# A casting load issued at the head of the kernel instead of inside its loop: 3x3 convolution by row-Winograd on one core

## The chip, the cores and the metric

The kernel runs on one core of a Trainium2 chip. The metric is the device time of one execution, in microseconds. The profile adds one profiled execution, read by its span (from the first to the last instruction) and by what each engine and each transfer queue did in it. Engines are named as in the profile: PE (TensorE), DVE (VectorE), ACT (ScalarE), POOL (GpSimd) and SP (SyncE, which here only issues transfers).

## The reference

A 3x3 convolution with padding 1. The input has 16 images of 64 channels, 64 x 64 pixels, the output 16 images of 128 channels, all float32.

```python
batch, c_in, h, w, c_out = 16, 64, 64, 64, 128
x_pad = np.pad(x, ((0, 0), (0, 0), (1, 1), (1, 1)), mode='constant')
# for every image b, output channel co, input channel ci, kh, kw in 0..2:
output[b, co] += weight[co, ci, kh, kw] * x_pad[b, ci, kh:kh+h, kw:kw+w]
```

The input is 16.8 MB and the output 33.6 MB.

## The kernel before

**Tiling.** Two images are worked on together. A pair's input is one tile of 128 partitions (2 images x 64 channels) by 64 x 64 pixels, and there are eight pairs, numbered 0 to 7. Two output rows are computed together: with the weight rows G0, G1, G2 of the filter, the products of G1 with the sum of two neighbouring input rows (`ss`, fp16) are common to both, and the combined weights G2-G1 and G0-G1 make up the rest from the input rows themselves (`xs`, fp16). Each pair is done in four blocks of eight row pairs. In a block, PE makes three groups of products (L150): U from `ss`, then A and B from `xs`, each for both images. ACT copies U from PSUM (L164), DVE adds it to A (L174) and to B (L177) into two output tiles `ot`, one for each image. A pair therefore needs its `ss` before its first product, and its `xs` right after.

**Where the input comes from.** There are two ways in.

- Pairs 0 to 3 are loaded as float32 by SP (L45 and L49), at the very start, into tiles of the pool `opool` that later hold outputs. POOL makes `ss` from the float32 tile (L76; for pair 0 it is DVE), and ACT casts the tile to `xs` (L101 for pair 0; L169 in the last two blocks of the pair before for 1 to 3).
- Pairs 4 to 7 are loaded by POOL with a casting load: the transfer reads float32 and writes fp16 straight into an `xs` tile (`load`, L65 to L67). POOL makes `ss` from that.

**Pools.** `xpool` has five fp16 tiles of input. The first four are named for pairs 0 to 3 before anything is loaded (L63); the load of pair 4 takes the fifth. Each later load takes the tile that has been in use longest: pair 5 that of pair 0, pair 6 that of pair 1, pair 7 that of pair 2, and it waits until the pair before has been used up. `opool` has eight tiles, `spool` three for `ss`.

**Order.** Instructions marked `keep` stay in the order in which they are written. On POOL, this order is: cast of the weights (L61), the two weight differences (L96, L97), the load of pair 4 (L98), and then for each pair p of the main loop the sums of pair p+1 (two instructions, L114) and, from p = 1 on, the load of pair p+4 (L116). POOL executes its instructions one after the other, so a load that waits for its tile holds up the sums behind it, and sums that wait for their input hold up the load behind them.

**Queues.** SP issues the weights, the four float32 loads, and then a store of each pair's first image (L181). ACT issues the stores of each pair's second image, one block later (L171, from the list `held`). The last pair is stored in two halves for each image. POOL issues only casting loads. The profile shows SP's transfers as q1, ACT's as q10 and POOL's as q0. All three run on the same 16 DMA engines.

Of the kernel before, what the change touches and what calls it, by code (L numbers as in the profile page):

```python
# [13 lines left out]
def kernel(  # L14
# [10 lines left out]
    NP = B // 2  # L25
# [6 lines left out]

    const = ctx.enter_context(tc.tile_pool(name="const", bufs=1))
    psum = ctx.enter_context(tc.tile_pool(name="psum", bufs=8, space=bass.MemoryType.PSUM))
    xpool = ctx.enter_context(tc.tile_pool(name="xpool", bufs=5))
    opool = ctx.enter_context(tc.tile_pool(name="opool", bufs=8))
    spool = ctx.enter_context(tc.tile_pool(name="spool", bufs=3))
    upool = ctx.enter_context(tc.tile_pool(name="upool", bufs=4))
# [26 lines left out]
    def load(p):  # L65
        xs[p] = xpool.tile([128, H, W], F16, tag="xs", name="xs")
        keep(nc.gpsimd.dma_start(xs[p], x_rows[128 * p : 128 * p + 128, :, :]))  # L67
# [3 lines left out]
    def sums(eng, p, src, lo, n):  # L71
        if p not in ss:
            ss[p] = spool.tile([128, H // 2, W], F16, tag="ss", name="ss")
        v = src.rearrange("p (j i) c -> p j i c", i=2)
        keep(
            eng.tensor_add(  # L76
                ss[p][:, lo : lo + n, :], v[:, lo : lo + n, 0, :], v[:, lo : lo + n, 1, :]
            )
        )
# [5 lines left out]
    def wrow(i):  # L85
        return Wt[:, i, :, :].rearrange("p t c -> p (t c)")
# [9 lines left out]
    keep(nc.gpsimd.tensor_sub(wrow(G21), wrow(G2), wrow(G1)))  # L96
    keep(nc.gpsimd.tensor_sub(wrow(G01), wrow(G0), wrow(G1)))  # L97
    load(4)  # L98
    for n, (lo, hi) in enumerate(cuts):
        sums(nc.vector, 0, x0, RB * n, RB)  # L100
        keep(nc.scalar.copy(xs[0][:, lo:hi, :], x0[:, lo:hi, :]))  # L101
# [3 lines left out]
    def store(eng, p, b2, ot, lo, hi):  # L105
        return eng.dma_start(
            out_rows[2 * p + b2, :, lo:hi, :],
            ot.rearrange("p j i c -> p (j i) c")[:, lo:hi, :],
        )

    for p in range(NP):
        if p + 1 < NP:
            for lo in (0, 16):
                sums(nc.gpsimd, p + 1, xf.get(p + 1, xs[p + 1]), lo, 16)  # L114
        if p > 0 and p + 4 < NP:
            load(p + 4)  # L116
        ots = [
            opool.tile([128, H // 2, 2, W], F32, tag="ot", name="ot") for _ in range(2)
        ]
        for blk in range(4):  # L120
            j0 = blk * RB

            def group(wi_rows):

                tiles = [
                    psum.tile([128, RB, W], F32, tag="acc", name="acc") for _ in range(2)
                ]
                n = 3 * len(wi_rows)
                i = 0
                for wi, off in wi_rows:  # L130
                    for kw in (1, 0, 2):
                        c_lo, c_hi = max(0, 1 - kw), min(W, W + 1 - kw)
                        for b2 in range(2):
                            p0 = 64 * b2
                            lo, hi = j0, j0 + RB
                            if off is None:
                                rhs = ss[p][p0 : p0 + 64, lo:hi, c_lo + kw - 1 : c_hi + kw - 1]
                            else:
                                while 2 * lo + off < 0:
                                    lo += 1  # L140
                                while 2 * (hi - 1) + off > H - 1:
                                    hi -= 1
                                first = 2 * lo + off
                                last = 2 * (hi - 1) + off
                                rhs = xs[p][
                                    p0 : p0 + 64,
                                    first : last + 1 : 2,
                                    c_lo + kw - 1 : c_hi + kw - 1,
                                ]
                            nc.tensor.matmul(  # L150
                                tiles[b2][:, lo - j0 : hi - j0, c_lo:c_hi],
                                Wt[p0 : p0 + 64, wi, kw, :],
                                rhs,
                                start=i == 0,
                                stop=i == n - 1,
                            )
                        i += 1
                return tiles

            U = group([(G1, None)])  # L160
            us = []
            for b2 in range(2):
                ut = upool.tile([128, RB, W], F32, tag="ut", name="ut")
                keep(nc.scalar.copy(ut, U[b2]))  # L164
                us.append(ut)
            if p + 1 in xf:
                q = p + 1
                for lo in {2: (0, 16), 3: (32, 48)}.get(blk, ()):
                    keep(nc.scalar.copy(xs[q][:, lo : lo + 16, :], xf[q][:, lo : lo + 16, :]))  # L169
            while held:  # L170
                keep(store(nc.scalar, *held.pop(0)))  # L171
            A = group([(G21, 1), (G0, -1)])
            for b2 in range(2):
                nc.vector.tensor_add(ots[b2][:, j0 : j0 + RB, 0, :], A[b2], us[b2])  # L174
            Bt = group([(G01, 0), (G2, 2)])
            for b2 in range(2):
                nc.vector.tensor_add(ots[b2][:, j0 : j0 + RB, 1, :], Bt[b2], us[b2])  # L177
            parts = {3: (0, 64)} if p < NP - 1 else {1: (0, 32), 3: (32, 64)}
            if blk in parts:
                lo, hi = parts[blk]  # L180
                store(nc.sync, p, 0, ots[0], lo, hi)  # L181
                held.append((p, 1, ots[1], lo, hi))
# [32 lines left out]
```

## Time and profile before

| What | us |
|---|---|
| median of 3 runs (126.5 to 126.59) | 126.5 |
| the profiled execution's own time | 126.56 |
| its span | 124.8 |
| PE busy | 108.2 |
| DVE busy | 82.8 |
| ACT busy | 52.0 |
| POOL busy | 36.2 |

The profiled execution stands 0.06 us above the median, and 1.8 us of it lie outside the span. PE starts on the main products at 9.92 us, and each pair takes 12.81 us on it: the pairs start at 9.92, 22.74, 35.54, 48.35 and so on. A busy time is the sum of an engine's instructions; it doesn't tell which of them the end waited for. That is read from the chain of waits and from the rows of the slices, where each digit is the busy share of 1/40 of the span. The input read is 17.07 MB with the weights, the output written 33.55 MB, together 406 GB/s over the span. In the queue lines a casting load counts with the bytes that it writes, half of those that it reads.

### The profile page before, as it was taken

The page shows a single profiled execution, that of the slowest core. Times are in us where ns is not written, and L with a number is a line of the kernel's source. Part 1 is how long each engine was busy: PE and PEld are TensorE (multiplying, and loading weights), DVE is VectorE, ACT ScalarE, POOL GpSimd, SP SyncE. Part 2 cuts the span into 40 slices and gives each one's busy share as a digit, 9 for nine tenths or more (in the row PEclk, how much of TensorE's full clock was granted, in tenths as well). Part 3 has the DMA queues.
Part 4 walks back from the last instruction along what each step waited for, and adds up shares of the span by engine and source line. Part 5 has one row for each costly group of instructions (what it writes and reads, how often), then busy time and mean ns, then how long its engine had stood idle before and what let it go on. Part 6 is the DMA issues. An engine that isn't in the chain of part 4 may idle for free.

```text
span 124.8 us, 2437 instructions
## 1 busy us (share of the span) xinstructions
PE 108.2 (87%) x988; PEld 49.3 (40%) x988; DVE 82.8 (66%) x133; ACT 52.0 (42%) x84; POOL 36.2 (29%) x27
## 2 busy tenths in 40 slices
PE   0699999999999999999999999999999999990000
PEld 0433444444444444444444444444444444440000
DVE  0016787878878787877777778777877787685000
ACT  4319749833993399333333333333333333330000
POOL 2360086294799202920067000940000000000000
PEclk9999999999999999999999999999999999999555
DMA  6899999999999999999999999999999999999991
GB/s 173 362 436 407 297 323 349 425 315 415 397 349 368 305 376 373 360 334 362 381 347 360 334 344 412 431 431 425 425 441 420 436 415 425 436 412 418 436 402 74
DMA packets 3898, 46.57 MB, mean 373 GB/s; under 512 B 432, under 2 KB 432, under 8 KB 560
## 3 DMA queue, kind: packets, MB, share of 16 engines
q1 hardware_dynamic: 2016, 25.46, 49.5%
q10 hardware_dynamic: 1296, 16.78, 31.6%
q0 software_dynamic: 576, 4.19, 16.1%
q8 instruction: 7, 0.11, 0.3%
q14 instruction: 3, 0.02, 0.0%
HBM read 17.07 MB, written 33.55 MB: 406 GB/s over the span
## 4 chain that ended last, share of the span: by engine, by line
PE 86%; DMA 2%; DVE 1%; issue 1%; POOL 1%; DVEq 0%
PE acc L150 81%; PE warm L56 4%; DMA w_raw<-in_weight_dram 2%; PE wp L93 1%; DVE ot L174 1%; POOL w L61 1%; DVE ot L177 0%; DVEq L210 0%; DVEq L174 0%
## 5 line engine op out<-in xcount | busy, mean ns | idle before, releaser
L150 PE MATMUL acc<-xs,Wt 64*128 64x504 f16 (+3 forms) x768 | 87.0, 373 | 0.0
L150 PEld LDWEIGHTS <-Wt 64*128 64x128 f16 x960 | 46.8, 94 | 56.2 <-issue 0.8
L164 ACT COPY ut<-acc 128x512 f32<-128x512 f32 x64 | 34.3, 588 | 52.9 <-issue 32.1
L174 DVE TENSOR_TENSOR ot<-acc,ut 128x512 f32<-128x512 f32 x64 | 41.2, 686 | 22.6 <-PE acc L150 18.3
L177 DVE TENSOR_TENSOR ot<-acc,ut 128x512 f32<-128x512 f32 x64 | 41.1, 684 | 0.0
L150 PE MATMUL acc<-ss,Wt 64*128 64x504 f16 (+1 forms) x192 | 26.0, 377 | 0.0
L76 POOL TENSOR_TENSOR ss<-xs 128x1024 f16<-128x1024 f16 x8 | 16.8, 2124 | 20.2 <-DMA xs<-in_x_dram 20.2
L76 POOL TENSOR_TENSOR ss<-xf 128x1024 f16<-128x1024 f32 x6 | 14.1, 2361 | 13.6 <-DMA xf<-in_x_dram 13.6
L169 ACT CAST xs<-xf 128x1024 f16<-128x1024 f32 x12 | 12.0, 1058 | 0.0
L76 DVE TENSOR_TENSOR ss<-x 128x512 f16<-128x512 f32 x4 | 2.5, 687 | 7.7 <-DMA x<-in_x_dram 7.7
L93 PE MATMUL wp<-ident,w 128*64 128x128 f16 x18 | 1.3, 328 | 4.3 <-POOL w L61 4.3
L101 ACT CAST xs<-x 128x1024 f16<-128x1024 f32 (+2 forms) x4 | 3.9, 1042 | 2.6 <-DMA x<-in_x_dram 2.6
L67 POOL DMA_DIRECT2D xs<-in_x_dram x4 | 2.4, 600 | 7.8 <-ACT xs L169 7.8
L56 PE MATMUL warm<-zeros 128*128 128x512 f16 x10 | 4.4, 631 | 0.0
L93 PEld LDWEIGHTS <-w 128*64 128x64 f16 x18 | 1.1, 210 | 4.3 <-POOL w L61 4.3
L94 ACT CAST Wt<-wp 128x384 f16<-128x384 f32 x3 | 1.2, 487 | 2.9 <-PE wp L93 2.9
L56 PEld LDWEIGHTS <-zeros 128*128 128x128 f16 x10 | 1.3, 143 | 2.3 <-issue 2.2
L94 ACT ACT_TABLE_LOAD x1 | 1.3, 1283 | 0.7 <-PEq L199 0.7
L96 POOL TENSOR_TENSOR Wt<-Wt 128x384 f16<-128x384 f16 x1 | 0.9, 907 | 1.7 <-ACT Wt L94 1.7
L61 POOL CAST w<-w_raw 128x576 f16<-128x576 f32 x1 | 0.7, 663 | 2.3 <-DMA w_raw<-in_weight_dram 2.3
L97 POOL TENSOR_TENSOR Wt<-Wt 128x384 f16<-128x384 f16 x1 | 0.9, 910 | 0.0
L51 DVE MEMSET zeros<- 128x256 uint32 x1 | 0.3, 272 | 0.9 <-PEq L199 0.9
(6 smaller groups left out, 0.9 us busy)
## 6 DMA issues: line engine op xcount, KB each, us to landing
out_dram<-ot SPq DMA_DIRECT2D x7, 2048.0 KB, 22.0
out_dram<-ot ACTq DMA_DIRECT2D x7, 2048.0 KB, 18.9
xf<-in_x_dram SPq DMA_DIRECT2D x3, 2048.0 KB, 22.1
xs<-in_x_dram POOLq DMA_DIRECT2D x4, 1024.0 KB, 23.4
x<-in_x_dram SPq DMA_DIRECT2D x1, 2048.0 KB, 7.6
out_dram<-ot SPq DMA_DIRECT2D x2, 1024.0 KB, 10.6
out_dram<-ot ACTq DMA_DIRECT2D x2, 1024.0 KB, 11.0
w_raw<-in_weight_dram SPq DMA_DIRECT2D x1, 288.0 KB, 2.8
```

The source lines that it names most:

```text
L56: keep(nc.tensor.matmul(warm, zeros[:, 0:128], zeros))
L61: keep(nc.gpsimd.tensor_copy(w16, w_raw))
L67: keep(nc.gpsimd.dma_start(xs[p], x_rows[128 * p : 128 * p + 128, :, :]))
L76: eng.tensor_add(ss[p][:, lo : lo + n, :], v[:, lo : lo + n, 0, :], v[:, lo : lo + n, 1, :])
L93: keep(nc.tensor.matmul(wp[q : q + 64, k * CO : k * CO + CO], w16[:, t::9], ident))
L94: keep(nc.scalar.copy(wrow(g), wp[:, 0 : 3 * CO]))
L101: keep(nc.scalar.copy(xs[0][:, lo:hi, :], x0[:, lo:hi, :]))
L150: nc.tensor.matmul(tiles[b2][:, lo - j0 : hi - j0, c_lo:c_hi], Wt[p0 : p0 + 64, wi, kw, :], rhs, start=i == 0, stop=i == n - 1,)
L164: keep(nc.scalar.copy(ut, U[b2]))
L169: keep(nc.scalar.copy(xs[q][:, lo : lo + 16, :], xf[q][:, lo : lo + 16, :]))
L174: nc.vector.tensor_add(ots[b2][:, j0 : j0 + RB, 0, :], A[b2], us[b2])
L177: nc.vector.tensor_add(ots[b2][:, j0 : j0 + RB, 1, :], Bt[b2], us[b2])
```

## The change

The pool of fp16 input tiles has six tiles instead of five. The load of pair 5 is issued directly behind that of pair 4, ahead of the main loop, and takes the sixth tile. The loop issues only the loads of pairs 6 and 7, at the same places as before (p = 2 and p = 3). Because of the sixth tile, these two take other tiles than before: pair 6 that of pair 0, pair 7 that of pair 1.

```diff
-    xpool = ctx.enter_context(tc.tile_pool(name="xpool", bufs=5))
+    xpool = ctx.enter_context(tc.tile_pool(name="xpool", bufs=6))
...
     load(4)
+    load(5)
     for n, (lo, hi) in enumerate(cuts):
         sums(nc.vector, 0, x0, RB * n, RB)
...
-        if p > 0 and p + 4 < NP:
+        if p > 1 and p + 4 < NP:
             load(p + 4)
```

The order of instructions on PE, DVE, ACT and SP is the same in both kernels. On POOL it changes as follows: the issue of load 5 moves from between the sums of pairs 2 and 3 to directly behind that of load 4.

## The prediction

> **What bounds the kernel now.** I read the chain of waits first, because it names what ended last. Its shares say TensorE:
>
> ```profile
> PE 86%; DMA 2%; DVE 1%; issue 1%; POOL 1%; DVEq 0%
> ```
>
> The page's slices and queue shares qualify this. The PE row is full from the third slice to the 36th (about 112 us), then there are 12 us in which only transfers run; the DMA row is full nearly everywhere:
>
> ```profile
> PE   0699999999999999999999999999999999990000
> DMA  6899999999999999999999999999999999999991
> ...
> q1 hardware_dynamic: 2016, 25.46, 49.5%
> q10 hardware_dynamic: 1296, 16.78, 31.6%
> q0 software_dynamic: 576, 4.19, 16.1%
> ```
>
> q1 carries what SP issues, q10 what ACT issues, q0 the casting loads that POOL issues. Together they fill 97.2% of the span on all 16 engines, 121.3 of 124.8 us. The missing 3.5 us lie mostly at the two ends: a share of 0.11 in the first 2 us, and 0.88 and 0.16 in 120 to 124. One casting load costs 16.1% x 124.8 / 4 = 5.0 us of all 16 engines, a 2 MB store 31.6% x 124.8 / 8 = 4.9 us (q10 carries eight stores' worth).
>
> So there are two limits, and they nearly coincide at the end. The transfers that close the kernel are issued here (SP, then ACT) and land 9.9 us later each, by the DMA view of the last stretch, at 123.25 and 123.85:
>
> ```profile
> 113.35 0.33 SPq L106 DMA_DIRECT2D out_dram<-ot  x1
> 113.95 0.34 ACTq L106 DMA_DIRECT2D out_dram<-ot  x1
> ```
>
> These two 1 MB stores need 4.9 us of engine time together, so most of the 9.9 us is start-up and backlog of earlier stores. How much is start-up: ACT's first store is issued at 24.30 into an empty queue, and the queues' view of 24 to 28 us has packets of q1 alone. Start-up is thus at least 28.0 - 24.3 = 3.7 us. If backlog vanished, the last pair could start at 113.35 + 3.7 = 117.05, take 4.9 us, and land about 1 us later (the time between data and landing; estimated from the 0.95 us between 123.85 and the end of the span): 123.0 instead of 123.85. TensorE and issue times would then hold the end, so relieving the transfers can win at most some 0.85 us; delaying TensorE costs nearly microsecond for microsecond.
>
> The timeline of POOL shows what the moved load stands behind:
>
> ```profile
> 7.63 0.70 POOL L67 DMA_DIRECT2D xs<-in_x_dram  x1
> 16.19 4.69 POOL L76 TENSOR_TENSOR ss<-xf 128x1024 f16<-128x1024 f32 x2 [7.86 <-DMA xf<-in_x_dram]
> 24.30 4.69 POOL L76 TENSOR_TENSOR ss<-xf 128x1024 f16<-128x1024 f32 x2 [3.42 <-DMA xf<-in_x_dram]
> 28.93 0.57 POOL L67 DMA_DIRECT2D xs<-in_x_dram  x1
> 31.84 4.68 POOL L76 TENSOR_TENSOR ss<-xf 128x1024 f16<-128x1024 f32 x2 [2.35 <-DMA xf<-in_x_dram]
> 36.48 0.57 POOL L67 DMA_DIRECT2D xs<-in_x_dram  x1
> 37.07 4.20 POOL L76 TENSOR_TENSOR ss<-xs 128x1024 f16<-128x1024 f16 x2
> 49.09 0.57 POOL L67 DMA_DIRECT2D xs<-in_x_dram  x1 [7.83 <-ACT xs L169]
> ```
>
> Adding the times to landing that the DMA view gives for each (14.8, 19.8, 27.0 and 29.0 us), loads 4 to 7 land at 22.4, 48.7, 63.5 and 78.1: they leave q0 one after the other. The POOL waits date the landings of the f32 inputs: pair 1 at 16.19, pair 2 at 24.30, pair 3 at 31.84.
>
> Last, stretches of the span with the share of the DMA engines and the rate:
>
> ```profile
> 24.00:25.50 1.50, 1.50 (x18) 0.72 (x16) 0.90 (x3) 0.70 (x2) 1.20 (x1) 1.00 1.01 426
> 25.50:28.00 2.50, 2.50 (x26) 1.14 (x24) 1.89 (x4) 1.07 (x2) 2.50 (x2) 1.00 1.05 295
> ```
>
> The last two columns are share and GB/s. From 25.5 to 28 the engines are occupied but move 295 instead of 426 GB/s, with q1 (the load of pair 3) alone: 2.5 x (1 - 295/426) = 0.77 us are lost. It is the one hole in the middle of the span. Casting loads also lower the printed rate, because they are counted as the 1 MB written; but q0 has no packet in this stretch.
>
> **The change, step by step.** The profiled execution took 126.56 us (span 124.8); the median of the runs is 126.5, 0.06 below.
>
> *The issue moves on POOL.* One 0.57 us issue leaves 28.93, another goes in at about 8.33. POOL idles 7.86 us before 16.19, so the addition is covered. SP's and ACT's queues keep their order. Cost 0.
>
> *Load 5's transfer.* It waits in q0 behind load 4, so until 22.4 nothing differs: pair 1 lands at 16.19 and its sums end at 20.88, ahead of TensorE's pair 1 at 22.74. From 22.4 it shares the engines with the load of pair 2, which has 1.9 us left. Bounds for that landing: 24.30 if the queued load starts late, 26.2 if the rest takes twice as long. I take 26.2, because q0 and q1 had 39.2% and 61.8% of the engines in 12 to 24 us, most of which they shared. Pair 2's sums then end at 30.9; TensorE needs them at 35.54. Cost 0, with 4.6 us to spare.
>
> *The load of pair 3.* Lower bound: 31.84 as now. Upper bound: all of load 5 (5.0 us) and all of ACT's first store (4.9 us) go ahead: 31.84 + 9.9 = 41.7. Sharing in turn puts it near 38, since load 5 finishes within that time anyway and the store takes only its turns; I take 38. The sums of pair 3 end at 42.7 (46.4 at the worst), TensorE needs them at 48.35; ACT casts that tile from 43.80. Cost 0 at either end; the cover is 5.7 us, 1.9 us at the worst. Nothing else is behind POOL's wait except loads 6 and 7 and later sums.
>
> *Load 6* is behind those sums, issued at 42.7 instead of 36.48 (bounds 36.5 and 46.4). Before, it left q0 only after 48.7; now it starts about 4 us after issue, near 47, so it lands close to the old 63.5 (bounds 55 and 65). Its sums could start as late as 86.8 - 4.2 = 82.6 (pairs start 12.81 us apart on TensorE). Cost 0. *Load 7* now takes the tile of pair 1, free since 35.5, so its 7.83 us wait goes; it follows the sums of pair 4, at 43.3 + 4.2 = 47.5 against 49.09. Next on POOL are the sums of pair 5, which TensorE wants at 74. Worth 0.
>
> *Stores.* SP's first store is behind pair 3's load in q1 and so some 6 us later, landing near 52 instead of 45.7. Its tile is written again by pair 4, from 61 on. ACT's stores gain in the same stretch. Cost 0.
>
> *The transfers as a whole.* No packet is added or removed. The engines were full before and stay full, so an earlier load only changes places with other transfers. The unknown is the 0.77 us hole: the second queue that now runs in it may fill it (-0.77), leave it (0), or suffer too (+0.8, when two reading streams lose what one lost). The nearest row with two reading queues, the queues' view of 12 to 24 us, has 4.13 MB, of which 0.98 MB by q0, whose reads are twice that: (4.13 + 0.98) MB / 12 us = 426 GB/s, a full rate without a hole. The cause of the hole itself no view names, and it may come again whoever runs. Between the two I take 0.
>
> Sum: 126.56 + 0 = 126.5 at the median.
>
> The Trainium skill, page "DMA: Bandwidth & Descriptors", section "Latency and other measured facts", speaks against the change here: it gives an HBM access latency of 0.2 us on average and 2 us at high load. By that rule a second reading stream could lengthen the hole rather than fill it, the second rival below; no run here shows it, and the full rate in 12 to 24 us is against it.
>
> **The rivals.**
>
> *The hole fills (faster).* The engines find q0's packets while q1's are slow. For it: the hole is a stretch with one active queue. Against: one queue alone ran at 418 GB/s in 4 to 8 us, so one queue is not the cause by itself. Time: 126.56 - 0.77 = 125.8; the limit at the end allows 125.7.
>
> *The hole grows (slower).* Place: 25.5 to about 38, while pair 3's load and load 5 both read beside new stores. Decisive point: whether the share stays full while the rate, casting bytes counted twice, falls below some 400. Twice the loss gives 126.56 + 0.8 = 127.3.
>
> *Pair 3 arrives too late (slower).* If its load lands after 43.66, TensorE waits for the sums, and the last stores go out later by the same time. Landing at 46 would give 126.5 + 2.3 = 128.8. Against it: even the upper bound above is 41.7.
>
> *The change frees TensorE.* The 7.83 us wait on POOL and waits for casting loads (20.2 us in total) look large, but TensorE ran without a gap from 9.99 to 111.4 on the chain. Nothing there can be won; this falls under no change.
>
> **How the numbers follow.** About 0.2% (0.25 us) is what a measurement of this kernel tells from no change. No change 0.45, 126.5. Hole fills 0.31, 125.8. Hole grows 0.19, 127.3. Pair 3 late 0.05, 128.8. Small reorderings in the last stores can shift single engines' ends (share 0.88, then 0.16 in the last 4 us) by a few tenths either way; that is inside these. The range goes from 125.6 to 127.4, over the first three; the no-change case alone is 126.25 to 126.75.
>
> **What would show it.** POOL: two issues at 7.6 and 8.3, no wait before load 7, the last sums near 78. Pair 3's sums start near 38 and TensorE still has no gap. In 24 to 28 us q0 and q1 both move packets; the rate there decides between the first rivals. The last stores are issued at 113.35 and 113.95 as now. I would be wrong if TensorE stops before 48.35, if those stores are later, or if the summed queue shares fall in the middle of the span.

## The result and the profile after

The changed kernel takes 126.97 us (median of 6 runs, 126.84 to 127.19), the kernel before 126.51 in the same comparison (126.38 to 126.59). The ratio is 1.0039, with a 95% interval of 1.0026 to 1.0051: slower by 0.46 us. (Ratios and their intervals, here and below, take only the runs within 1.5% of the same kernel's fastest run; medians and ranges are of all runs.) The forecast was no change. The time lies inside the range, but it moved the way for which the forecast had a chance of 0.24.

The page of the changed kernel answers line by line to the one before. The chain of waits, the slices and the queues' shares hardly differ:

```profile
PE 86%; DMA 2%; DVE 1%; issue 1%; POOL 1%; DVEq 0%
...
PE   0599999999999999999999999999999999990000
DMA  5999999999999999999999999999999999999980
...
q1 hardware_dynamic: 2016, 25.46, 48.9%
q10 hardware_dynamic: 1296, 16.78, 31.5%
q0 software_dynamic: 576, 4.19, 16.2%
```

The span is 125.2 us, so the queues' 96.6% are 120.9 us of all 16 engines, against 121.3 before. The transfers thus needed no more engine time in sum, and yet the kernel ends later. The timeline of POOL shows the order that the change asked for:

```profile
7.80 1.23 POOL L67 DMA_DIRECT2D xs<-in_x_dram  x2
15.56 4.70 POOL L76 TENSOR_TENSOR ss<-xf 128x1024 f16<-128x1024 f32 x2 [6.53 <-DMA xf<-in_x_dram]
25.66 4.68 POOL L76 TENSOR_TENSOR ss<-xf 128x1024 f16<-128x1024 f32 x2 [5.40 <-DMA xf<-in_x_dram]
39.15 4.68 POOL L76 TENSOR_TENSOR ss<-xf 128x1024 f16<-128x1024 f32 x2 [8.81 <-PE acc L151]
43.78 0.57 POOL L67 DMA_DIRECT2D xs<-in_x_dram  x1
44.38 4.21 POOL L76 TENSOR_TENSOR ss<-xs 128x1024 f16<-128x1024 f16 x2
48.53 0.57 POOL L67 DMA_DIRECT2D xs<-in_x_dram  x1
```

Both loads are issued at the head, and load 7 no longer waits. (The wait before 39.15 is put down to PE, which had long been done with that tile; what came last is the load of pair 3.) Two places in the stretches of the span differ. First, in the middle, the kernel before and then the changed one (the last two columns are the share of the DMA engines and GB/s):

```profile
34.00:48.00 14.00, 14.00 (x136) 6.37 (x132) 10.59 (x17) 9.27 (x15) 7.24 (x5) 1.00 1.02 358
```

```profile
34.00:48.00 14.00, 14.00 (x134) 6.32 (x132) 10.47 (x18) 9.27 (x15) 8.83 (x5) 1.00 1.00 424
```

Before, load 5 ran here beside the stores: q0 had 32.5% of the engines. In the changed kernel load 5 is over by 34 us and load 6 starts at 48, so the stores (and at first the end of pair 3's load) are alone. Second, the very end, again before and then after:

```profile
121.00:122.00 1.00, 0.00 (x0) 0.00 (x0) 0.00 (x0) 0.00 (x0) 0.00 (x0) 0.50 0.72 303
122.00:123.00 1.00, 0.00 (x0) 0.00 (x0) 0.00 (x0) 0.00 (x0) 0.00 (x0) 0.50 0.30 123
123.00:124.00 1.00, 0.00 (x0) 0.00 (x0) 0.00 (x0) 0.00 (x0) 0.00 (x0) 0.50 0.02 8
```

```profile
121.00:122.00 1.00, 0.00 (x0) 0.00 (x0) 0.00 (x0) 0.00 (x0) 0.00 (x0) 0.50 0.61 254
122.00:123.00 1.00, 0.00 (x0) 0.00 (x0) 0.00 (x0) 0.00 (x0) 0.00 (x0) 0.50 0.22 90
123.00:124.00 1.00, 0.00 (x0) 0.00 (x0) 0.00 (x0) 0.00 (x0) 0.00 (x0) 0.50 0.04 16
```

After the change the engines as a whole are done sooner (0.61 and 0.22 against 0.72 and 0.30), but more is left past 123 us. The queues' view of 121 to 124 us, in 40 slices, shows what is left, before and then after:

```profile
DMA  7599295909590722972070020002000000000000
```

```profile
DMA  7758772559252922270002000200020002000000
```

In the changed kernel there is one lone packet after another from the 19th slice on: a single engine, still working after the other 15 have ended. The kernel waits for it. In the kernel before, the lone packets start later and are fewer.

The trace's records of single packets say when it fell behind. (A packet is here one row of a transfer as the trace lists it.) A 16 KB packet of a store takes 611 or 624 ns. In 34 to 48 us of the changed kernel 18 of 360 packets took 634 to 667; before it was 1 of 246. They are not spread over the engines; each starts where the one before it ended:

```
start us / ns, changed kernel, packets of q1 and q10 lasting 634 to 690 ns
36.94 667   37.60 653   38.25 644   38.89 634   39.52 658   40.18 661
40.84 644   41.48 639   42.12 644   42.76 644   43.40 653   44.05 652
44.69 644   45.33 644   45.98 666   46.64 644   47.28 644   47.92 644
```

This is one engine's sequence of packets, on average some 36 ns longer than the 611 of the other 15. From the end of load 7, near 77 us, to 113 us the same runs through both kernels. While a load is under way beside the stores, it stops.

Followed in this way to the end, from one packet to the next, it is also the sequence that ends last: at 123.35 us in the kernel before, 0.52 after the next engine, and at 123.82 in the changed one, 1.16 after the next. On its last stretch it no longer lags. From about 2 us after TensorE's last product, the 8 KB packets of the last pair take 309 ns on it as on the others, although stores run alone there too.

### The profile page after: what moved, and what is told of

The parts are those of the page before. It is cut to its first block, busy times and chain, and to the rows that moved or that the text cites. A ratio compares the mean times of both kernels' runs of the same rounds, so it can differ in the third digit from the quotient of the medians.

```text
span 125.2 us, 2436 instructions
## 1 busy us (share of the span) xinstructions
PE 108.3 (87%) x988; PEld 48.9 (39%) x988; DVE 82.8 (66%) x133; ACT 52.0 (42%) x84; POOL 36.3 (29%) x27
## 4 chain that ended last, share of the span: by engine, by line
PE 86%; DMA 2%; DVE 1%; issue 1%; POOL 1%; DVEq 0%
PE acc L151 81%; PE warm L56 3%; DMA w_raw<-in_weight_dram 2%; PE wp L93 1%; DVE ot L175 1%; POOL w L61 1%; DVE ot L178 0%; DVEq L211 0%; DVEq L175 0%
## 6 DMA issues: line engine op xcount, KB each, us to landing
out_dram<-ot SPq DMA_DIRECT2D x7, 2048.0 KB, 24.7
```

## The experiments

Theory S, formed from this: while stores run with no load beside them, one DMA engine needs some 36 ns more for each 16 KB packet; the kernel ends with that engine; loading early leaves more stores alone. Its rivals: the sixth tile (L), the later start of TensorE (2), the early transfer by what it meets at the head (E, H), the gap that it leaves in q0 (G).

The count that S turns on, from the records of each profiled execution: 16 KB packets of stores lasting 634 to 690 ns in 34 to 114 us, and what they took beyond 615 ns. Packets that ran at the same time as one of the sequence, and so on other engines, are left out: 5 in the changed kernel, 3 with the later TensorE, 15 with loads 6 and 7 early, all near 103 to 105 us. The hole is what packets took beyond 624 ns in 20 to 40 us, as a mean over the 16 engines. The last column is the median less the median of the kernel before in the same comparison; the other columns are of one profiled execution each, and the end of a single one can stand some tenths off (the later TensorE: last packet 0.38 later, median no later).

```
kernel                            long  beyond  hole  last packet   time
                                        us      us    ends, us      us
before                             54   1.80    0.94    123.35
six tiles only                     53   1.76    0.74    123.46     -0.11
before, later TensorE              53   1.74    0.98    123.73     -0.07
changed                            73   2.39    0.67    123.82     +0.46
changed, again                     73   2.42    0.60    123.63     +0.37
load 5 behind pair 1's sums        69   2.25    0.76    123.87     +0.36
load 4 later                       58   1.91    1.19    123.69     +0.37
changed, load 6 in halves          59   1.96    0.66    123.38     +0.08
before, load 6 in halves           41   1.27    0.60    123.10     -0.24
before, all stores on SP           75   2.44    0.98    124.48     +0.82
loads 6 and 7 early too            77   2.52    0.64    123.99     +2.85
```

### The changed kernel again, one part alone, and a later TensorE

No edit in the first.

> The changed kernel itself, for a second profile. If the +0.46 us belong to the change, it stands at 126.9 to 127.1 again. Theory 1 (one DMA engine ends late: the mean engine is no later, only the last one is): the last stores are issued some 0.2 us later than in the kernel before, the rate in 112 to 120 us is the same, and the last landing is late by more than the issue is. Theory 2 (the end follows TensorE, which started 0.25 us later because the weights landed 0.18 us later): the weights land late here too (2.97 us after issue against 2.79).

127.0 us against 126.63, ratio 1.0038 (1.0013 to 1.0063). The weights land late here too (about 3.0 us after issue), but on the chain of waits TensorE's main products start at 9.59 us, not at 9.99 as in the kernel before. The last stores are issued here,

```profile
113.16 0.33 SPq L107 DMA_DIRECT2D out_dram<-ot  x1
113.76 0.34 ACTq L107 DMA_DIRECT2D out_dram<-ot  x1
```

0.19 us earlier than in the kernel before, where theory 1 expected them 0.2 later too. The last packet still ends 0.28 later, and 0.90 after the next engine.

The sixth tile alone, against the kernel before:

```diff
-    xpool = ctx.enter_context(tc.tile_pool(name="xpool", bufs=5))
+    xpool = ctx.enter_context(tc.tile_pool(name="xpool", bufs=6))
```

> Six tiles, every load issued where it was. Theory L (the sixth tile alone costs, by other addresses of the tiles behind it): 126.9 to 127.1 as the whole change. Theory E (the early transfer costs, whatever tile it takes): 126.5, within 0.15 us; load 7 no longer waits, and nothing else moves.

126.52 us, ratio 0.9996 (0.9973 to 1.0019). The tile costs nothing; theory L falls.

Load 5 between the two places, against the changed kernel:

```diff
     load(4)
-    load(5)
...
+        if p == 0:
+            load(5)
         if p > 1 and p + 4 < NP:
```

> Six tiles, load 5 issued behind the sums of pair 1 (about 20.9 us) instead of at the head (8.3) or behind those of pair 2 (28.9). Its packets start about 4 us later, near 25, when the load of pair 3 is under way and the load of pair 2 has landed. Theory E, if what costs is the sharing with the load of pair 2 or pair 3: between 126.5 and 127.0, nearer to 127.0 if pair 3 is what matters. Theory L: 126.9 to 127.1 again.

126.99 us, ratio 1.0041 (1.0007 to 1.0075). Load 5 now misses pair 2's load altogether and costs the same: meeting it is not what costs. It still meets the load of pair 3.

TensorE later, in the kernel before:

```diff
-    spin(10)
+    spin(12)
```

> The kernel before with twelve instead of ten warm-up products, so that TensorE starts the main products some 0.5 to 0.9 us later (one warm-up product takes about 0.44 us in the stretch). Theory 2 (the end follows TensorE): the time grows by as much, to 127.0 to 127.4. If the transfers hold the end alone, it stays at 126.5 within 0.15 us.

126.56 us, ratio 1.0003 (0.998 to 1.0027). The dose was smaller than expected: the two products cost 0.14 us, and with the weights landing later by about 0.1 the main products began at 10.17 us instead of 9.92. But this is just the delay that the changed kernel shows. Its last stores are issued here (timeline, changed kernel):

```profile
113.61 0.33 SPq L107 DMA_DIRECT2D out_dram<-ot  x1
114.21 0.34 ACTq L107 DMA_DIRECT2D out_dram<-ot  x1
```

and those of the kernel before with the later TensorE here:

```profile
113.60 0.33 SPq L106 DMA_DIRECT2D out_dram<-ot  x1
114.20 0.34 ACTq L106 DMA_DIRECT2D out_dram<-ot  x1
```

Same issue times, no loss. Theory 2 falls, and a quarter of a microsecond on TensorE is free.

### The gap in q0, load 4, and the size of the stores

The changed kernel with loads 6 and 7 one pair earlier:

```diff
-        if p > 1 and p + 4 < NP:
-            load(p + 4)
+        if p > 0 and p + 5 < NP:
+            load(p + 5)
```

> The changed kernel with loads 6 and 7 issued one pair earlier each, so that they follow load 5 in q0 without the gap of 34 to 48 us. Theory S (where stores run without a load beside them, one of the 16 DMA engines needs some 36 ns more for each 16 KB packet, and the end is that engine's; the early load leaves more such stores): the gap goes, but stores alone begin near 62 us instead of 76, so as many packets are long as in the changed kernel, 65 to 75 of them, and the time is 126.9 to 127.1. Theory G (the gap in q0 itself costs, by the start-up of a load into an empty queue): 126.5.

129.35 us in the median, with runs from 127.19 to 131.53, ratio 1.0124 (1.0086 to 1.0162). Neither number came. The gap is gone, and 77 packets are long, about as many as in the changed kernel, as S wants, but most of the loss is another mechanism. SP's first store, behind pair 3's load in q1 and beside the loads in q0, now lands so late that DVE waits for it (chain of waits, then timeline of DVE):

```profile
23.48 30.64 DMA out_dram<-ot
```

```profile
54.25 1.29 DVE L175 TENSOR_TENSOR ot<-acc,ut 128x512 f32<-128x512 f32 x2 [4.58 <-DMA out_dram<-ot]
```

and TensorE stops with it. So the price of the rest can't be read from this kernel, and theory G is not settled by it.

The kernel before with load 4 later:

```diff
-    load(4)
...
-        if p > 0 and p + 4 < NP:
+        if p + 4 < NP:
             load(p + 4)
```

> The kernel before with load 4 moved the other way: out of the head to behind the sums of pair 1 (about 20.9 us), so that most of its transfer runs beside stores; five tiles, all else as it was. Theory S: more stores have a load beside them, so fewer long packets (40 to 48 instead of 54 to 60) and the slowest engine gains 0.3 to 0.6 us; other engines end within 0.5 us of it, so 126.1 to 126.4. Theory H (what costs is only that load 5 meets the loads of pairs 2 and 3 at the head): load 4 doesn't meet load 5 there either, so 126.5.

126.87 us, ratio 1.0035 (1.0011 to 1.0059), slower where S had been read to say faster, and not the 126.5 of theory H either. The count explains why the reading was wrong: 58 long packets, not 40 to 48. Load 4 now runs partly beside pair 3's load, and loads 5 to 7 end where they did, near 77 us. And the hole of 25.5 to 28 us, with a load in q0 in it, is deeper, as the stretches of this kernel show:

```profile
24.00:25.50 1.50, 1.50 (x18) 0.76 (x14) 0.89 (x3) 0.56 (x2) 1.43 (x2) 1.00 1.12 224
25.50:28.00 2.50, 2.50 (x26) 1.35 (x24) 1.77 (x4) 1.07 (x2) 0.22 (x1) 1.00 1.01 134
```

134 GB/s, or at most 268 if all of it were a casting load's bytes counted twice. The hole took 1.19 us of each engine instead of 0.94. Together with 0.11 us more in long packets that is 0.36, and the last packet ends 0.34 later. By this sum most of the loss of this kernel comes from the hole.

Stores in halves, first in the kernel before, then in the changed one:

```diff
-            parts = {3: (0, 64)} if p < NP - 1 else {1: (0, 32), 3: (32, 64)}
+            parts = {1: (0, 32), 3: (32, 64)}
```

> The kernel before with every pair stored in halves, as the last pair is now: 8 KB packets instead of 16 KB. Of the last pair's 512 packets only some eight are longer than 320 ns against 309 for the rest. Theory S, if the long packets come from the 16 KB form: no engine lags, and the end is 0.3 to 0.6 us earlier, 125.9 to 126.2. If the engine lags for stores of any size (18 ns on 309): 126.5. The stores are issued earlier by half a pair, which by itself moves nothing in the middle of the span, where the transfers are behind.

> The changed kernel with every pair stored in halves. Theory S with 16 KB packets as its condition: without them the early load costs nothing, so the same time as the kernel before with halves, within 0.15 us. If the early load costs for another reason: 0.4 to 0.5 us more than that kernel.

127.72 us, ratio 1.0088 (1.0051 to 1.0126), and 128.06, ratio 1.0129 (1.009 to 1.0167). A miss: one engine lags with 8 KB packets too, by some 22 ns each on 309, once stores run alone. (In the last pair of the kernel before, only two of the 512 packets are longer than 320 ns, not eight.) It stops lagging near 115 us, when TensorE has done its last product, which comes 2.4 us later than in the kernel before. The early load still costs 0.34 us by the medians, though the two ranges of runs overlap (127.62 to 128.14 and 127.9 to 129.17). Halves cost in themselves. The loads are over by 64 and 67 us instead of 77, two 8 KB packets take 618 ns where one of 16 KB takes 611, and DVE waits for a store here as well (timeline of DVE in the first of the two kernels):

```profile
67.98 0.69 DVE L174 TENSOR_TENSOR ot<-acc,ut 128x512 f32<-128x512 f32 x1 [2.73 <-DMA out_dram<-ot]
```

TensorE stops with it, and the last stores are issued 2.3 us later than in the kernel before, at 115.61 and 115.65 by SP. So these two kernels don't give the price of the lag.

### More and less cover for the stores

If S holds, the time must follow the length of the stretch in which loads run beside stores, in both directions and without touching the head. A casting load in two parts of 32 rows has packets of half the size, and so a smaller share in each round:

```diff
-        keep(nc.gpsimd.dma_start(xs[p], x_rows[128 * p : 128 * p + 128, :, :]))
+        step = H // 2 if p == 6 else H
+        for r in range(0, H, step):
+            keep(
+                nc.gpsimd.dma_start(
+                    xs[p][:, r : r + step, :], x_rows[128 * p : 128 * p + 128, r : r + step, :]
+                )
+            )
```

> The changed kernel with load 6 issued as two casting loads of 32 rows each, so that its packets read 8 KB instead of 16 KB and it takes half as large a share beside the stores, about 24 us instead of 14; load 7 follows later, and stores without a load beside them begin near 86 us instead of 77. Theory S (the engine that lags while stores run without a load beside them sets the end): 12 to 16 long packets fewer, and the time is back near the kernel before, 126.4 to 126.7. If the early transfer costs by something that happens at the head: 127.0 as the changed kernel.

126.70 us against 126.62, ratio 1.0013 (0.9992 to 1.0034). With load 5 still at the head and the gap of 34 to 48 us still in q0, 59 long packets, and the loss is gone within what was measured. The spans alone say the same: 124.7 to 125.0 us here, 124.9 to 125.6 in the twelve runs of the changed kernel again. So theories G and H fall as the main cause: what happens at the head is unchanged, and only the cover at the far end is longer. The long packets of 34 to 49 us are still there (18); those saved are later ones.

> The kernel before with load 6 as two halves. Theory S: stores without a load beside them begin near 86 us instead of 77, the long packets go from 54 to 60 down to some 40 to 45, the lagging engine gains 0.5 us, of which other engines, up to 0.5 us ahead of it, leave 0.1 to 0.4: 126.1 to 126.4. Otherwise 126.5.

126.38 us, ratio 0.9991 (0.9967 to 1.0016). The sign is as S wants, though the interval doesn't exclude no change. Long packets: 41. The stretches of this kernel show that a load still runs from 76 to 90 us (372 GB/s with the casting bytes counted once, where the kernel before has 430 with stores alone), and that nothing is left past 123 us:

```profile
76.00:90.00 14.00, 14.00 (x134) 7.46 (x132) 11.17 (x18) 4.29 (x8) 0.93 (x1) 1.00 1.02 372
...
123.00:124.00 1.00, 0.00 (x0) 0.00 (x0) 0.00 (x0) 0.00 (x0) 0.00 (x0) 0.50 0.00 0
```

It gains less than the 0.5 us taken off the slow engine, since others end at 122.97 and 123.10. This is the one version that came out below both kernels, by an amount that these runs don't resolve.

Less cover, in the kernel before:

```diff
-                keep(store(nc.scalar, *held.pop(0)))
+                keep(store(nc.sync, *held.pop(0)))
```

(the same in the two places where `held` is emptied).

> The kernel before with ACT's stores issued by SP at the same place in the program. One store queue instead of two shares the engines with a load half and half, so loads 5 to 7 are over sooner, near 64 us instead of 77, and more stores run alone. Theory S: some 18 long packets more and 0.4 to 0.7 us more time, 126.9 to 127.2. Otherwise 126.5, or another time by something that the trace shows as an idle stretch of the transfers.

127.44 us, ratio 1.0073 (1.0036 to 1.0109). The loads are over at 64 us, 75 packets are long, and the end of the span has the form of the changed kernel's, only later (stretch of 123 to 124 us):

```profile
123.00:124.00 1.00, 0.00 (x0) 0.00 (x0) 0.00 (x0) 0.00 (x0) 0.00 (x0) 0.50 0.06 25
```

The engine with the long packets ends last, 1.29 us after the next. The loss is larger than 0.64 us more in long packets gives. What the rest is, this run doesn't tell.

## Why the prediction was wrong

**The step that failed** is "The transfers as a whole": "The engines were full before and stay full, so an earlier load only changes places with other transfers." The sum over 16 engines did stay (120.9 us against 121.3), but two things in the step were wrong. A packet's duration is not independent of what runs beside it: stores without a load beside them cost one engine some 36 ns a packet while TensorE was at work. And the end is the slowest engine's, not the mean one's. In the changed kernel the mean engine ended at 122.03 us instead of 122.21, and the last one at 123.82 instead of 123.35. Load 5 had covered stores in 34 to 48 us; at the head it runs beside other loads, where nothing needs cover. That made 18 of the 19 additional long packets (19 instead of 1 before 49 us). The sum that the step should have made: 2.39 - 1.80 = 0.59 us more on the slow engine, less 0.27 by which the hole became smaller, 0.32; the last packet ended 0.47 later, so 0.15 us stay open. (The hole is a mean; the records don't name the engine, so its share of it isn't known. In the other kernels where this engine ends last, the same sum comes out between right and 0.45 us too small.)

**The hole** was the right unknown, but it was the smaller one, and its sign was right for the first rival: a second queue in it took part of it away, 0.67 instead of 0.94 us. The HBM latency at high load that the prediction takes from the Trainium skill (page "DMA: Bandwidth & Descriptors", section "Latency and other measured facts") as an argument for a deeper hole is not borne out by that pair; a deeper hole did come with load 4 moved (1.19), so a second reading queue can go either way, and what makes the hole is open.

**"Delaying TensorE costs nearly microsecond for microsecond"** was wrong for the first quarter of a microsecond, which is free. The sign "if those stores are later" thus appeared, by 0.26 us in the profiled execution, without being the cause: in the second profile they were 0.19 us earlier, and the loss was there. The limit of 0.85 us was worked out with 1 us from the last data to its landing; in the kernel before it was 0.5 (123.35 to 123.85).

**"Its tile is written again by pair 4, from 61 on"** was wrong as well. DVE's first add of pair 3 waits for SP's first store. In the changed kernel that store, issued at 23.96, landed 24.7 us later, at 48.66; the add runs at about 50.7. The cover was 2 us, not 9, and with two more loads early it was used up. That this step cost nothing was luck: had the store landed near 52, as forecast, DVE would have waited for it.

**Right** were the steps on POOL and TensorE: issues at 7.80 to 9.03, pair 2's sums at 25.66 (26.2 forecast), pair 3's at 39.15 (38), load 6 at 43.78 (42.7), load 7 without a wait at 48.53 (47.5), its sums at 78.54, and no gap on TensorE. All of that was hidden, as predicted. Where a slower result was forecast at all, it was for the hole and for a late pair 3, neither of which happened. That 126.97 us lies in the range is luck too: its upper end was the deeper hole.

**What can be called shown, and what not.** That the early transfer costs, and not the tile or TensorE, is shown by undoing them one by one. That the loss comes from the stores left without a load is shown by the changed kernel with load 6 in halves, which gets the time back with the head as it was. The other direction is weaker: in the kernel before, the gain isn't resolved, and with all stores on SP the loss is larger than the count gives. That one engine lags there and ends last is read from the packets, in the kernel before, both profiles of the changed one, load 5 behind pair 1's sums and all stores on SP; with six tiles only, another engine ends last. Why it lags, and which it is, stays open. S as worded is also too wide: the lag stops with TensorE's work, and whether that work or DVE's is a condition of it was not tested. The Trainium skill, page "DMA: Bandwidth & Descriptors", section "Latency and other measured facts", says that engines 7 and 15 are usually slower and gives as a best guess that descriptor rings used by POOL's transfers make their ports busier. By that guess the lag would come with casting loads. Here it is the other way round: it stops while q0 has a load, and one long packet of 246 falls into 34 to 48 us of the kernel before, where q0 is active.

## What to carry to other kernels

Where transfers fill the whole span, a moved load need not be free, even if nothing waits for it: what it ran beside may go slower without it. Look at which stretches hold reads and writes together, and which are left with writes alone. Read the end of such a kernel by its last slices, whether all engines stop together or one goes on alone; only the last one counts, and a sum of queue shares doesn't show it. Cover for a tile ends where the program writes it next, so look up that wait before counting on it.

## What was not expected of the hardware

One of the 16 DMA engines took mostly 634 to 667 ns for 16 KB packets of stores where the others took 611 or 624, whenever stores ran without a load and TensorE was at work, in every kernel traced here with whole stores, and apart from the hole and a moment near 103 to 105 us hardly otherwise. A 2 MB transfer has its first packet late when other queues keep the engines busy: ACT's first store, issued at 24.30 into an empty queue, at 28.59, and the one issued at 101.14, whose queue ran empty at 103.9, at 105.10, so about 4 us. The first load, issued at 1.17 while the engines were idle, had its first packet at 2.69. And each of the seven 16 KB fetches of instructions takes some 0.9 us on one engine (0.88 to 1.02 in the kernel before), more than the whole loss looked for here.
